# A 512-token trunk layer: the embedding product made by Strassen's scheme inside the output projection

## The chip, the core and the metric

The kernel runs on one NeuronCore of a Trainium2 chip. Five engines take part. TensorE (PE in the profile) multiplies into PSUM, which has eight banks of 128 x 512 fp32 values. VectorE (DVE) and ScalarE (ACT) work elementwise on SBUF and PSUM, GpSimd (POOL) issues DMAs with addition and does a little arithmetic, and SyncE (SP) issues plain DMAs. Each engine runs its own instructions strictly in program order and waits on semaphores for the others. The metric is the device time of one execution in microseconds. The kernel before takes 790.21 us (median of three runs, 790.07 to 790.22).

## The reference, cut to what matters

```python
D_MODEL, SEQ, PLE_DIM = 2048, 512, 256
def reference(x, p, ...):
    hn = rmsnorm(x, norm_g[0])
    x = x + swa_mixer(hn, ...)            # ends in (out * silu(gate)) @ w_out, 2048 x 2048
    emb = p[0] @ ple_proj[0]              # 512 x 256 @ 256 x 2048: the embedding
    g = sigmoid(rmsnorm(x, ple_norm[0]) @ ple_gate[0])   # 2048 x 2048: the gating product
    x = x + emb * g
    return rmsnorm(x, final_g)
```

All of it is fp32. The embedding `emb` needs only the inputs `p` and `ple_proj`, so it can be made at any time before the gating uses it.

## The kernel before, in words

**Products in three parts.** Each fp32 operand is split into a high half rounded to fp32r and a low half that holds the rest; `mm3` (L123) makes a product from three matmuls, high by high, high by low and low by high (L126 to L128 in the profile). A split costs one ACT cast and one DVE subtraction.

**Four large stages.** Input projections and attention come first (to about 450 us). The output projection `w_out` follows, then the gating product `ple_gate`, then the last rows with their stores. The output projection and the gating product are each done by a Strassen-like scheme of seven products of half size, in the order `ORDER_OUT = ORDER_PLE = (1, 7, 6, 5, 3, 4)` (L664) for six of them, and the seventh by a second level of small products (`SMALL`, L666: at which piece of which product a small one is put in). Product p has two column halves jj; a unit is written (p, jj), and has four pieces m = 0 to 3, so (6, 0, 1) is piece 1 of unit (6, 0). A piece is 128 x 1024 of weights, 512 KB, and feeds 12 matmuls 512 wide (`unit`, L997): two 128-row halves, two blocks of 128 tokens, three matmuls each. Units of products 6, 5 and 3 go on adding to the banks of product 1 (`chain`, L978).

**The pieces.** `Pieces` (L720) holds one list of specifications over both stages. When piece i is asked for (`get`, L779), `ahead` (L768) issues the DMA loads of the next three to six pieces on SP (L747, tile `braw`), and splits every piece up to i + 2: cast (L754, tile `bhi`) and subtraction (L755, tile `blo`). The tiles `bhi` and `blo` have three buffers each, so the cast of piece n waits until PE has finished piece n - 3. What is called piece n below is the n-th entry of this list: pieces 0 to 7 belong to product 1, 8 to 15 to product 7, and piece 16 opens product 6.

**Activation forms.** The moving side is the token operand, split the same way and formed as sums of quarters (`Forms`, L836; casts L867, subtractions L868, tiles `fho`/`flo` for the output projection, `fhg`/`flg` for the gating). They are made one product ahead, two buffers to the ring, so a form's cast waits for the piece that used its buffer last.

**The embedding.** `p` transposed is loaded and split once (L1205 to L1208, `pTh`, `pTl`). `ple_proj` comes as eight pieces of 128 x 2 x 512 in the same list, put between the units of the gating (`EMBEDS`, L827, `add_embeds`, L797). `embed` (L1211) makes a block of 128 tokens by 512 columns with 6 matmuls into a PSUM bank `e`. `gated` (L1217) takes the sigmoid on ACT (L1223), multiplies it by the bank on DVE (L1225), and adds the result to x, on DVE (L1229) or by an accumulating DMA on POOL (L1227). ACT then takes squares and their sums (L1240). The last four blocks are made in the tail by `block` (L1383), which multiplies by the pieces of product 4, then calls `embed`, for the tokens 256 to 511; the last of them is done in two strips of 288 and 224 columns on a bank that ACT has opened with the negative of what is to be subtracted (`opened_bank`, L1377).

**What sets the order.** In the output projection DVE, ACT and POOL follow a scheduler that reorders the instructions of each engine from the order of the code; from product 7 of the gating on, all engines follow the code (L1318). PE and SP follow the code throughout the stages in question here.

## Time and profile before

| what | value |
|---|---|
| median of three runs | 790.21 us (790.07 to 790.22) |
| the profiled execution, its own time | 789.45 us |
| its span, first to last instruction | 787.7 us |
| granted TensorE clock, mean | 0.996 |
| PE busy | 778.7 us, 99% |
| DVE busy | 607.9 us, 77% |
| ACT busy | 507.0 us, 64% |
| POOL busy | 139.6 us, 18% |
| output projection, first matmul of product 1 | at 450.57 us of the span |
| last matmul starts | at 779.3 us of the span |

The busy time of PE counts overlapping matmuls once: the matmuls are pipelined, one of 512 columns lasts about 0.39 us in the records and the next starts 0.23 us after it. Rows of the timeline read: start, duration, engine, line, operation, output and inputs, shape, and in brackets the idle time before it and what ended that. A row of the groups ends with the busy time, the mean of one in ns, and the idle time before. A row of the windows gives, for each engine in turn, busy us and instruction count, then the granted clock, the share of time that the 16 DMA engines are busy and GB/s.

### The profile page before, as it was taken

Reading aid. Unit: us, or ns where it says so; the run is one execution under the profiler, and the core shown is the slowest. Engines: PE = TensorE matmul, PEld = TensorE weight load, DVE = VectorE, ACT = ScalarE, POOL = GpSimd, SP = SyncE. Lnnn points to the kernel's source line nnn. Section 1 sums busy time; section 2 is a strip of 40 time slices with the busy share of each in tenths; the row PEclk is TensorE's granted clock in tenths of the full one; section 3 lists DMA queues with packets and bytes.
Section 4 is the critical chain, followed back from the end, with each engine's and each line's share of the span. In section 5 each row is a group of like instructions: output and inputs, shape, how many; then the busy total and the mean of one; then the engine's idle time right before and its main releaser. Section 6 shows DMA issues by size and latency. Waiting matters only on the chain. (4 is left out here: it accounts for less than half of the span.)

```text
span 787.7 us, 11098 instructions
## 1 busy us (share of the span) xinstructions
PE 778.7 (99%) x3726; PEld 651.8 (83%) x3726; DVE 607.9 (77%) x1037; ACT 507.0 (64%) x1064; POOL 139.6 (18%) x258
## 2 busy tenths in 40 slices
PE   9999999999999999999999999999999999999995
PEld 8888888888888888888888888888888888888885
DVE  4547697876877688777777898778879589877896
ACT  6743576666767576766666754456689666656953
POOL 0201423132223323122222200000000022202000
PEclk9999999999999999999999999999999999999998
DMA  9978999999999989999997489667873899979723
GB/s 346 294 206 298 194 274 298 292 280 269 280 275 258 271 232 309 256 289 263 282 258 197 136 320 383 207 209 238 270 265 108 292 290 262 247 239 251 208 86 129
DMA packets 47817, 198.07 MB, mean 251 GB/s; under 512 B 7104, under 2 KB 8128, under 8 KB 42000
## 3 DMA queue, kind: packets, MB, share of 16 engines
q1 hardware_dynamic: 38736, 151.95, 55.7%
q0 software_dynamic: 9024, 45.41, 30.0%
q8 instruction: 29, 0.48, 0.3%
q14 instruction: 28, 0.23, 0.1%
HBM read 189.16 MB, written 71.35 MB: 331 GB/s over the span
## 5 line engine op out<-in xcount | busy, mean ns | idle before, releaser
L755 DVE TENSOR_TENSOR blo<-braw,bhi 128x1024 fp32r<-128x1024 f32 x108 | 131.5, 1222 | 37.3 <-ACT bhi L754 36.4
L754 ACT CAST bhi<-braw 128x1024 fp32r<-128x1024 f32 x108 | 113.4, 1051 | 55.9 <-PE o L128 25.9
L126 PE MATMUL gps<-xh,whi 128*128 128x512 f32 x256 | 100.0, 390 | 0.0
L127 PE MATMUL gps<-xl,whi 128*128 128x512 f32 x256 | 99.9, 390 | 0.0
L128 PE MATMUL gps<-xh,wlo 128*128 128x512 f32 x256 | 99.7, 390 | 0.0
L126 PE MATMUL qps<-xh,whi 128*128 128x512 f32 x224 | 87.8, 392 | 0.0
L127 PE MATMUL qps<-xl,whi 128*128 128x512 f32 x224 | 87.4, 390 | 0.0
L128 PE MATMUL qps<-xh,wlo 128*128 128x512 f32 x224 | 87.3, 390 | 0.0
L110 DVE TENSOR_TENSOR wlo<-wraw,whi 128x1024 fp32r<-128x1024 f32 x60 | 73.5, 1227 | 2.8 <-ACT whi L109 2.7
L570 POOL TENSOR_SCALAR_AFFINE_SELECT own<-r 64x512 fp32r<-64x512 f32 (+1 forms) x48 | 32.5, 677 | 242.9 <-DVE r L560 237.2
L126 PE MATMUL o<-bhi,fho 128*128 128x512 f32 x192 | 74.8, 390 | 0.0
L128 PE MATMUL o<-bhi,flo 128*128 128x512 f32 x192 | 74.8, 389 | 0.0
L127 PE MATMUL o<-blo,fho 128*128 128x512 f32 x192 | 74.7, 389 | 0.0
L556 ACT CAST r<-pt 128x256 fp32r<-128x256 f32 x64 | 23.9, 374 | 68.8 <-PE pt L551 68.6
L109 ACT CAST whi<-wraw 128x1024 fp32r<-128x1024 f32 x60 | 62.3, 1040 | 4.6 <-issue 4.1
L126 PE MATMUL g<-bhi,fhg 128*128 128x512 f32 x160 | 62.7, 392 | 0.0
L128 PE MATMUL g<-bhi,flg 128*128 128x512 f32 x160 | 62.3, 389 | 0.0
L127 PE MATMUL g<-blo,fhg 128*128 128x512 f32 x160 | 62.3, 389 | 0.0
L128 PEld LDWEIGHTS gps<-xh,wlo 128*128 128x128 f32 x256 | 48.1, 188 | 10.3
L126 PEld LDWEIGHTS gps<-xh,whi 128*128 128x128 f32 x256 | 48.1, 188 | 9.1
L127 PEld LDWEIGHTS gps<-xl,whi 128*128 128x128 f32 x256 | 48.1, 188 | 8.8
L560 DVE TENSOR_TENSOR r<-pt,r 128x256 fp32r<-128x256 f32 x56 | 23.7, 424 | 41.0 <-ACT r L556 40.3
(244 smaller groups left out, 1789.3 us busy)
## 6 DMA issues: line engine op xcount, KB each, us to landing
wraw<-in_w_gate_in SPq DMA_DIRECT2D x32, 512.0 KB, 8.3
w_out<-in_w_out POOLq DMA_DIRECT2D x32, 512.0 KB, 9.0
braw<-w_out SPq DMA_DIRECT2D x32, 512.0 KB, 4.8
wraw<-in_w_q SPq DMA_DIRECT2D x28, 512.0 KB, 6.6
braw<-in_w_out SPq DMA_DIRECT2D x22, 512.0 KB, 4.1
braw<-in_ple_gate SPq DMA_DIRECT2D x22, 512.0 KB, 5.4
xw<-in_first SPq DMA_DIRECT2D x14, 640.5 KB, 6.7
w_out<-in_w_out SPq DMA_DIRECT2D x16, 512.0 KB, 10.2
```

Source lines behind the costliest of these rows:

```text
L109: nc.scalar.copy(hi, raw)
L110: nc.vector.tensor_sub(lo, raw, hi.bitcast(F32))
L126: nc.tensor.matmul(ps, sh, mh, start=first, stop=False, skip_group_check=more)
L127: nc.tensor.matmul(ps, sh, ml, start=False, stop=False, skip_group_check=more)
L128: nc.tensor.matmul(ps, sl, mh, start=False, stop=last, skip_group_check=more)
L556: nc.scalar.copy(rh, src)
L560: nc.vector.tensor_sub(rl, src, rh.bitcast(F32))
L570: nc.gpsimd.affine_select(out=flat(own), in_=flat(r).bitcast(F32), pattern=[[0, 8], [sign, HB]], compare_op=ALU.is_ge, fill=0.0, base=-HB ...
L754: nc.scalar.copy(hi, raw)
L755: nc.vector.tensor_sub(lo, raw, hi.bitcast(F32))
```

## The change

The eight `ple_proj` pieces, the split of `p` and the `e` banks leave the gating stage. A new class `Embedding` makes the same 512 x 2048 product inside the output projection, by Strassen's scheme with seven products in place of eight, in two column halves. Nine entries "emb" are put into the list of pieces, behind the pieces named in `EMBED_AT`: five of 1024 columns and four of 512. Their sums are prepared in the buffers `s1` and `s7` (free until the gating) by loads on SP, accumulating DMAs on POOL and four DVE additions (`embed_steps`); the forms of `p` are made in unit (7, 0) from `s2`. Each of the nine slots takes matmuls into pairs of banks from the tags "t" and "o", and sums are built by copying: ACT copies a bank into another bank (negated, to open it) or into SBUF. Each finished pair of blocks (128 x 2 x 512, 512 KB) is written to DRAM from `s2` by a POOL DMA (`keep`). There are 84 matmuls of 512 columns. In the gating each pair is loaded back by an SP DMA (`load_embeds`, tile tag "e", two buffers), at the pieces named in `embed_loads`, and the multiplication reads SBUF. The small products of the output projection move later (`SMALL`, `small_steps`). `fg` is allocated after product 3, since it shares its room with forms of `p`.

```diff
     SMALL = {
         "w_out": {
-            (5, 0): {1: [1], 3: [1]}, (5, 1): {1: [7], 3: [7]}, (3, 0): {1: [6], 3: [6]}, (3, 1): {1: [2], 3: [2]},
+            (5, 1): {2: [1], 3: [1]}, (3, 0): {0: [7], 1: [7], 3: [6]}, (3, 1): {0: [6], 1: [2], 3: [2]},
             (4, 0): {0: [5], 1: [5], 2: [4], 3: [4]}, (4, 1): {0: [3], 1: [3]},
...
             lo = wpool.tile([P, WE], F32R, tag="wlo", name=f"blo{i}")
-            nc.scalar.copy(hi, raw)
-            nc.vector.tensor_sub(lo, raw, hi.bitcast(F32))
+            n = raw.shape[-1]
+            nc.scalar.copy(hi[:, :n], raw)
+            nc.vector.tensor_sub(lo[:, :n], raw, hi[:, :n].bitcast(F32))
...
-                for of, j in EMBEDS.get((p, jj), ()) if nm == "ple_gate" else ():
-                    add_embeds(of, j)
         return at
 
     EMBEDS = {
-        (6, 1): [((1, 0), 0)], (5, 0): [((1, 1), 1), ((5, 0), 2)], (5, 1): [((5, 1), 3)],
-        (3, 0): [((3, 0), 2)], (3, 1): [((3, 1), 3)],
+        (6, 1): [(1, 0)], (5, 0): [(1, 1), (5, 0)], (5, 1): [(5, 1)], (3, 0): [(3, 0)], (3, 1): [(3, 1)],
     }
+
+    EMBED_AT = [
+        (6, 0, 1), (6, 0, 2), (6, 1, 0), (6, 1, 1), (6, 1, 3), (5, 0, 0), (5, 0, 2), (5, 0, 3), (5, 1, 1),
+    ]
...
-    fg = late.tile([P, D], F32, name="fg")
-    pTh = late.tile([P, 2, S], F32R, name="pTh")
-    pTl = late.tile([P, 2, S], F32R, name="pTl")
...
     small_steps = {
-        (6, 1, 2): 1, (5, 0, 0): 7, (5, 0, 2): 7, (5, 1, 0): 6, (5, 1, 2): 6, (3, 0, 2): 2, (3, 1, 0): 5, (3, 1, 2): 5,
+        (5, 0, 2): 1, (5, 1, 0): 7, (5, 1, 2): 7, (5, 1, 3): 6, (3, 0, 1): 6, (3, 0, 2): 2, (3, 1, 0): 5, (3, 1, 2): 5,
         (3, 1, 3): 4, (4, 0, 1): 3, (4, 0, 3): 3,
+    }
+
+    embeds = {
+        (c, jj): tc.dram_tile([P, 2, 512], F32, name=f"embeds{c}_{jj}") for c in (1, 5, 3, 4) for jj in range(2)
+    }
...
+            v1, v7 = flat(s1), flat(s7)
+            self.b1, self.b4, self.b5 = v7[:, :512], v7[:, 512:WE], v7[:, WE:]
+            self.b2, self.b3 = v1[:, :WE], v1[:, WE:]
+            self.to = [s2[:, n] for n in range(2)]
...
+            if step == "p":
+                load(self.to[1], a["pT"])
+            elif step == "forms":
+                self.make_forms()
+            elif step == "load0":
+                load(b4, src(1, 2, 0))
+                load(b31, src(2, 2, 0))
+                load(b1, src(1, 1, 0))
+                load(b20, src(2, 1, 0))
+            elif step == "sums0":
+                load(b50, src(2, 1, 0))
+                load(b51, src(1, 1, 1))
+                nc.vector.tensor_add(b30, b4, b31)
+                nc.vector.tensor_add(b21, b30, b1)
+                add(b4, src(1, 1, 0))
+                add(b50, b21)
+                B.base.update(zip(self.at, (b1, self.b2, self.b3, b4, b5)))
...
+        def times(self, q, piece, half, banks, first=False):
+            fh, fl = self.forms[q]
+            (bh, bl) = (v[half] for v in piece)
+            for tb in range(2):
+                mm3(banks[tb], fh[:, blk(tb)], fl[:, blk(tb)], bh, bl, first, True, True)
+
+        def bank_pair(self, name, tag):
+            return [bank(f"{name}{self.done}_{tb}", tag) for tb in range(2)]
+
+        def keep(self, c, jj, n, fill):
+            for tb in range(2):
+                fill(self.to[n][:, tb], tb)
+            nc.gpsimd.dma_start(embeds[c, jj], self.to[n])
+
+        def slot(self):
+
+            k = self.done
+            jj = 0 if k < 5 else 1
+            piece = B.get(self.at[k])
+            if k == 0:
+                self.left()
+            if k in (4, 8):
+                self.times(4, piece, 0, self.Z)
+                self.keep(4, jj if k == 8 else 0, 1, lambda to, tb: nc.scalar.copy(to, self.Z[tb]))
+            if k in (0, 4):
+                self.X = self.bank_pair("eX", "t")
+                self.times(1, piece, 1 if k else 0, self.X, True)
+                self.O = self.bank_pair("eO", "o")
+                for tb in range(2):
+                    nc.scalar.mul(self.O[tb], self.X[tb], -1.0)
+            elif k in (1, 5):
+                self.times(2, piece, 0, self.O)
+                self.times(6, piece, 1, self.X)
+                self.keep(1, jj, 0, lambda to, tb: nc.scalar.copy(to, self.O[tb]))
+                self.Y = self.bank_pair("eY", "o")
+                for tb in range(2):
+                    nc.scalar.copy(self.Y[tb], self.X[tb])
+            elif k in (2, 6):
+                self.times(7, piece, 0, self.Y)
+                self.times(3, piece, 1, self.X)
+                for tb in range(2):
+                    nc.scalar.copy(self.left_of[:, tb], self.Y[tb])
+                for tb in range(2):
+                    nc.scalar.copy(self.to[0][:, tb], self.X[tb])
+            elif k in (3, 7):
+                self.W = self.bank_pair("eW", "o")
+                self.times(5, piece, 0, self.W, True)
+                self.keep(5, jj, 1, lambda to, tb: nc.vector.tensor_add(to, self.W[tb], self.left_of[:, tb]))
+                self.keep(3, jj, 0, lambda to, tb: nc.vector.tensor_add(to, self.W[tb], to))
+                self.Z = self.bank_pair("eZ", "o")
+                for tb in range(2):
+                    nc.scalar.mul(self.Z[tb], self.left_of[:, tb], -1.0)
+            self.done += 1
+
+    embedding = Embedding(at_out["embed"])
+    embed_steps = {
+        (1, 1, 2): "p", (7, 0, 1): "forms", (7, 0, 3): "load0", (7, 1, 1): "sums0", (6, 0, 2): "load1", (6, 0, 3): "load2",
+        (6, 1, 0): "load3", (6, 1, 2): "sums1",
+    }
...
             def between(m, ps):
+                if (p, jj, m) in EMBED_AT:
+                    embedding.slot()
...
+                part = embed_steps.get((p, jj, step))
+                if part is not None:
+                    embedding.prepare(part)
...
-    pT = wpool.tile([P, WE], F32, tag="wraw", name="pT").rearrange("p (k t) -> p k t", k=2)
-    nc.sync.dma_start(pT, a["pT"])
-    nc.scalar.copy(pTh, pT)
-    nc.vector.tensor_sub(pTl, pT, pTh.bitcast(F32))
...
-    def embed(t, w, tag, c=slice(0, 512)):
-        e_ps = bank(f"e{t}_{done[t]}", tag)
-        for k in range(2):
-            mm3(e_ps[:, c], pTh[:, k, blk(t)], pTl[:, k, blk(t)], w[0][k][:, c], w[1][k][:, c], k == 0, k == 1)
-        return e_ps
-
-    def gated(t, j, zin, z, e_ps, c=slice(0, 512), share=1.0):
+    embed_of = {}
+
+    def load_embeds(c, jj):
+        t = embed_of[c, jj] = late.tile([P, 2, 512], F32, tag="e", name=f"e{c}_{jj}", bufs=2)
+        nc.sync.dma_start(t, embeds[c, jj])
+
+    embed_loads = {
+        (6, 1, 0): (1, 0), (6, 1, 2): (1, 1), (5, 0, 3): (5, 0), (5, 1, 3): (5, 1), (3, 0, 1): (3, 0), (3, 1, 1): (3, 1),
+        (3, 1, 3): (4, 0),
+    }
+
+    def gated(t, j, zin, z, e, c=slice(0, 512), share=1.0):
...
-        nc.vector.tensor_mul(z, e_ps[:, c], z)
+        nc.vector.tensor_mul(z, e[:, c], z)
...
+                if (p, jj, step) in embed_loads:
+                    load_embeds(*embed_loads[p, jj, step])
...
-            for (of, which), j in EMBEDS.get((p, jj), ()):
-                e = {}
-                w = B.get(at_ple["e", (of, which)])
-                for t in (2, 3) if of == 5 else (0, 1):
-                    e[t] = embed(t, w, "to"[which])
+            for of, which in EMBEDS.get((p, jj), ()):
+                e = {t: embed_of[of, which][:, t % 2] for t in ((2, 3) if of == 5 else (0, 1))}
...
-        e_ps = embed(2 + tb, w[jj], e_tag, c)
-        z = s2[:, jj, tb, c]
+        e, z = embed_of[4, jj][:, tb], s2[:, jj, tb, c]
...
+    load_embeds(4, 1)
```

The numbers behind an underscore in the following rows only keep tiles apart, and the number in `bhi15` is the piece's. In the kernel after, casts of pieces are L755 and those of forms L865.

First, ACT at the passage from product 7 to product 6 of the output projection, before. `fho5_00` to `fho5_11` are the four form casts of product 5; each waits for the piece that last used its buffer (`fho5_10` for piece 14).

```order
L754 CAST bhi13_5285<-braw13_5257 128x1024
L754 CAST bhi14_5308<-braw14_5281 128x1024
L867 CAST fho5_00_5431<-gate0_896 128x512
L754 CAST bhi15_5332<-braw15_5304 128x1024
L867 CAST fho5_01_5454<-gate0_896 128x512
L754 CAST bhi16_5356<-braw16_5259 128x1024
L867 CAST fho5_10_5497<-gate1_2333 128x512
L754 CAST bhi17_5374<-braw17_5283 128x1024
L867 CAST fho5_11_5520<-gate1_2333 128x512
L754 CAST bhi18_5392<-braw18_5306 128x1024
```

The same place after.

```order
L755 CAST bhi13_5306<-braw13_5278 128x1024
L755 CAST bhi14_5331<-braw14_5302 128x1024
L865 CAST fho5_00_5456<-gate0_896 128x512
L865 CAST fho5_01_5497<-gate0_896 128x512
L865 CAST fho5_10_5565<-gate1_2333 128x512
L755 CAST bhi15_5355<-braw15_5329 128x1024
L755 CAST bhi16_5383<-braw16_5280 128x1024
L755 CAST bhi17_5401<-braw17_5304 128x1024
L865 CAST fho5_11_5608<-gate1_2333 128x512
```

The casts of pieces 15 and 16 now stand behind `fho5_10`, where before they stood ahead of it.

Second, SP in the gating at the end of product 5, before (pieces 108 to 110 are the last of unit (5, 1), 112 is the first of product 3).

```order
L747 DMA braw109_7242<-ple_gate_5_1_2_832 128x1024
L747 DMA braw110_7262<-ple_gate_5_1_3_833 128x1024
L747 DMA braw111_7282<-in_ple_proj 128x2x512
L747 DMA braw112_7304<-in_ple_gate 128x1024
L747 DMA braw113_7330<-in_ple_gate 128x1024
L747 DMA braw114_7352<-in_ple_gate 128x1024
```

After, the numbers of the pieces are higher; 116 is the last of unit (5, 1) and 117 the first of product 3. `e5_0` is the first pair of the embedding for product 5, and takes the buffer that `e1_0` had.

```order
L747 DMA braw115_7398<-ple_gate_5_1_2_832 128x1024
L747 DMA braw116_7422<-ple_gate_5_1_3_833 128x1024
L1366 DMA e5_0_7445<-embeds5_0_5041 128x1024
L747 DMA braw117_7448<-in_ple_gate 128x1024
L747 DMA braw118_7471<-in_ple_gate 128x1024
L747 DMA braw119_7497<-in_ple_gate 128x1024
```

A load that waits for the second multiplication with `e1_0` on DVE now stands ahead of the loads of pieces 117 and 118.

Third, ACT from the casts of the first pieces of product 3 on, before.

```order
L1240 ACTIVATE s1_5039,ssq3_5038<-x1s_5033 128x512 x2
L754 CAST bhi113_7380<-braw113_7330 128x1024
L754 CAST bhi114_7400<-braw114_7352 128x1024
L1223 ACTIVATE s7_5041<-s7_5041,rstd2_6370 128x512
L867 CAST fhg4_00_7419<-hT0_6310 128x512
L762 CAST last0_7423<-grown72_6493 128x1024
L754 CAST bhi115_7429<-braw115_7378 128x1024
```

The same place after.

```order
L755 CAST bhi117_7499<-braw117_7448 128x1024
L755 CAST bhi118_7521<-braw118_7471 128x1024
L1379 ACTIVATE s7_5038<-s7_5038,rstd2_6595 128x512 x2
L1396 ACTIVATE s1_5036,ssq3_5035<-x1s_5033 128x512 x2
L755 CAST bhi119_7549<-braw119_7497 128x1024
L1379 ACTIVATE s7_5038<-s7_5038,rstd2_6595 128x512
L865 CAST fhg4_00_7568<-hT0_6535 128x512
L763 CAST last0_7572<-grown81_6714 128x1024
L755 CAST bhi120_7578<-braw120_7519 128x1024
```

Piece 112 of before is 117 of after. Two sigmoids and two squares now stand between the casts of the second and the third piece of unit (3, 0), and a sigmoid, a form and the first of the last pieces again before the fourth.

94 lines of the change are left out of this document (75 added, 19 removed).

## The prediction

> **What bounds the kernel now.** I read the page's busy times first, then the windows by stage, then the timeline where the change puts its work.
>
> ```profile
> PE 778.7 (99%) x3726; PEld 651.8 (83%) x3726; DVE 607.9 (77%) x1037; ACT 507.0 (64%) x1064; POOL 139.6 (18%) x258
> ```
> ```profile
> core 0: us, PE busy (x) PEld busy (x) DVE busy (x) ACT busy (x) POOL busy (x), PEclk, DMA share, GB/s
> 447.00:475.00 28.00, 28.00 (x126) 23.24 (x125) 27.95 (x33) 15.59 (x21) 2.12 (x2) 1.00 0.77 275
> 475.00:500.00 25.00, 25.00 (x112) 20.67 (x112) 22.18 (x27) 11.94 (x14) 0.00 (x0) 1.00 0.91 344
> 500.00:560.00 60.00, 60.00 (x266) 49.71 (x265) 46.65 (x52) 35.87 (x50) 0.00 (x0) 1.00 0.69 215
> ...
> 749.03:779.70 30.67, 30.57 (x163) 26.41 (x161) 28.26 (x47) 15.56 (x33) 1.91 (x3) 1.00 0.31 104
> ```
>
> The waits of PE over the whole span are one row, at the very start:
>
> ```profile
> PE warm_ps L141 <- PEq L1537: 0.9, 1, 0.9
> ```
>
> PE has no gap in any of these stretches: until 779.7 us every matmul follows the one before. So a matmul more costs its pitch, and a wait of PE, which now has none, costs its whole length. But in the last stretch DVE is busy for 28.26 of 30.67 us. There two engines are full at once, and taking work from one alone need not shorten it.
>
> **The change, term by term.** *Matmuls.* The embedding's own rows, ahead of 749.03 and from there on (L127 is a third of them):
>
> ```profile
> L127 PE MATMUL e<-blo,pTh x20: 389/389/389, 692.1 to 737.7; 128*128 128x512 f32 x20
> ...
> L127 PE MATMUL e<-blo,pTh x14: 273/389/389, 749.3 to 779.2; 128*128 128x512 f32 x10, 128*128 128x288 f32 x2, 128*128 128x224 f32 x2
> ```
> ```profile
> 488.63 0.62 ACT L867 CAST fho<-gate 128x512 fp32r<-128x512 f32 x1 [0.29 <-PE o L127]
> 488.65 0.39 PE L126 MATMUL o<-bhi,fho 128*128 128x512 f32 x1
> ...
> 491.35 0.62 ACT L867 CAST fho<-gate 128x512 fp32r<-128x512 f32 x1 [1.15 <-PE o L127]
> 491.37 0.39 PE L126 MATMUL o<-bhi,fho 128*128 128x512 f32 x1
> 491.60 0.39 PE L127 MATMUL o<-blo,fho 128*128 128x512 f32 x1
> 491.87 1.05 ACT L754 CAST bhi<-braw 128x1024 fp32r<-128x1024 f32 x1
> 492.95 1.23 DVE L755 TENSOR_TENSOR blo<-braw,bhi 128x1024 fp32r<-128x1024 f32 x1 [0.26 <-ACT bhi L754]
> ```
>
> The two PE rows at 488.65 and 491.37 open pieces 14 and 15 of the output projection: 12 matmuls in 2.72 us, a pitch of 0.227 us. The new scheme has 84 matmuls (7 products, 2 column halves, 2 token blocks, 3 parts), all where PE is full: +19.1 us. Removed are 60 early ones (3 x 20), 13.6 us, and 42 late ones: 30 wide at 0.227, 12 narrow at about 0.12 in proportion to their width, 8.2 us. Over the whole kernel that is 2.7 us less of PE. Whether the late 8.2 us come back is for DVE to say:
>
> ```profile
> 750.88 1.22 DVE L755 TENSOR_TENSOR blo<-braw,bhi 128x1024 fp32r<-128x1024 f32 x1
> 752.02 1.22 DVE L763 TENSOR_TENSOR low<-grown,last 128x1024 fp32r<-128x1024 f32 x1
> 753.15 1.22 DVE L755 TENSOR_TENSOR blo<-braw,bhi 128x1024 fp32r<-128x1024 f32 x1
> 754.29 0.68 DVE L1225 TENSOR_TENSOR s<-e,s 128x512 f32<-128x512 f32 x1
> ...
> 778.53 0.45 DVE L1472 TENSOR_TENSOR x1s<-x1s,fg 128x288 f32<-128x288 f32 x1
> 779.70 0.39 DVE L1225 TENSOR_TENSOR s<-e,s 128x224 f32<-128x224 f32 x1 [0.72 <-PE e L128]
> ```
>
> DVE runs here almost without a gap, and waits for PE once, for 0.72 us at the end. The last stores go out behind that work. What the change takes off DVE here are the subtractions of the last two embedding pieces (750.88 and 753.15, each 1.13 us to the next start) and that wait: 3.0 us come back. Bounds: 0.7 (the wait alone) and 8.2 (PE alone counts). I take 3.0 because DVE, not PE, has no room. Net: 19.1 - 13.6 - 3.0 = **+2.5 us** (-2.7 to +4.8).
>
> *Piece 15.* The order of ACT changes: the cast of piece 15 now stands behind `fho5_10`. The row at 491.35 is that form's cast: it waits for the second last matmul of piece 14, so it cannot move up. Today the cast and the subtraction behind it (491.87, 492.95) are those of piece 17, due later. In the new order the same two rows are those of piece 15, so its low half is ready at 492.95 + 1.23 = 494.18. PE needs it for the second matmul of piece 15, which now starts at 491.60. Stall: **+2.6 us**. Its load (two loads and two halves of `ple_proj`, 1 MB, are put ahead of it on SP) hides behind the same wait. Bounds: 2.3 and 3.0, by handoffs; piece 16 follows with 1 us in hand.
>
> *ACT copies and DVE sums.* The 28 bank copies are of this kind (the only rows of an ACT copy 512 wide out of PSUM):
>
> ```profile
> L1268 ACT ACTIVATE s<-g 128x512 f32<-128x512 f32 x4 | 2.3, 593 | 0.7 <-PE g L128 0.7
> ```
>
> 28 x 0.59 is 16.6 us. By the windows ACT has 13 us free in 475 to 500 and 24 us in 500 to 560. The cover is what a piece has in hand: that of piece 17 is ready at 494.18 by the rows above and needed at 491.60 + 2 x 2.72 = 497.04, so 2.9 us early. I cost the copies at nothing; a pair of them (1.2 us) ahead of a cast fits into the 2.9 us, two pairs and a sum do not quite, and then the piece behind is late. DVE is full in 447 to 475 and gets the form work of unit (7, 0): five operations of 512 columns (0.68) and five of 256,
>
> ```profile
> L560 DVE TENSOR_TENSOR r<-pt,r 128x256 fp32r<-128x256 f32 x56 | 23.7, 424 | 41.0 <-ACT r L556 40.3
> ```
>
> 5.5 us in all, spread over two units of 10.9 us each. I cost it at nothing, covered by the same 2.9 us and by DVE's 2.8 free us after 475; the upper end is 2.
>
> *Parking.* Each 512 KB store reads a buffer that ACT writes again. The squares of the output projection write the same `s2` and wait for the next to last store; the cast of a piece stands behind them on ACT. Near rows:
>
> ```profile
> braw<-in_ple_gate SPq DMA_DIRECT2D x22, 512.0 KB, 5.4
> ...
> braw<-small_ple_gate SPq DMA_DIRECT2D x8, 512.0 KB, 7.0
> ...
> x1s<-s POOLq DMA_DIRECT2D x8, 256.0 KB, 5.6
> ...
> out<-x1s SPq DMA_DIRECT2D x1, 512.0 KB, 3.5
> ```
>
> A store takes 3.5 to 5.6 us, from the sums of slot 7 to those squares PE runs two pieces and a slot, 5.4 to 6.8 us (a slot is 6 to 12 matmuls), and DVE's sums and another store come first. I take **+0.7 us** (0 to 4).
>
> *The gating.* The load of `e5_0` waits on SP until DVE is through with `e1_0`, and pieces 117 and 118 wait behind it. That product ends about 1 us after PE has done piece 112. The load of piece 117 then takes 5.4 to 7.0 us (the rows above), and one more load is ahead of it: 512 KB at 344 GB/s by 0.91 of the engines, 1.4 us where the engines are full, as they nearly are here. Behind it come, from these rows,
>
> ```profile
> L755 DVE TENSOR_TENSOR blo<-braw,bhi 128x1024 fp32r<-128x1024 f32 x108 | 131.5, 1222 | 37.3 <-ACT bhi L754 36.4
> L754 ACT CAST bhi<-braw 128x1024 fp32r<-128x1024 f32 x108 | 113.4, 1051 | 55.9 <-PE o L128 25.9
> ...
> L867 ACT CAST fhg<-hT 128x512 fp32r<-128x512 f32 x20 | 12.3, 613 | 4.7 <-DVE hT L855 2.6 <-PE g L127 2.1
> ...
> L1240 ACT ACTIVATE s<-x1s 128x512 f32<-128x512 f32 x15 | 9.4, 625 | 8.3 <-DVE x1s L1229 8.3
> ...
> L1223 ACT ACTIVATE s<-s,rstd 128x512 f32<-128x512 f32 x11 | 7.6, 718 | 6.9 <-DVE s L1399 5.0 <-DVE s L1274 1.9
> ...
> L1240 ACT ACTIVATION_READ_ACCUMULATOR s<-x1s 128x1 f32 x15 | 2.8, 186 | 0.0
> ...
> L1225 DVE TENSOR_TENSOR s<-e,s 128x512 f32<-128x512 f32 x15 | 10.0, 684 | 0.0
> ...
> L1274 DVE TENSOR_TENSOR s<-g,s 128x512 f32<-128x512 f32 x4 | 2.6, 682 | 0.0
> ```
>
> cast 1.05, subtraction 1.22, a product 0.68 and the read of the chain's bank 0.68, for which PE waits before it can go on with product 3 in that bank. In all 10.0 (without the load ahead) to 13.0 us, against the four pieces that PE has meanwhile, 10.9 us. Before, 12 to 24 embedding matmuls (2.7 to 5.4 us) stood between the units and gave room. I take the middle, 1.0 (0 to 2.1). From that read to the split of piece 120 runs a chain from ACT to DVE and back: two sigmoids 1.44, two squares 1.62, cast 1.05, subtraction 1.22, bank 0.68, sigmoid 0.72, form 0.61, two casts 2.10, subtraction 1.22, together 10.7, some 0.5 less since an operation starts before the one ahead of it is written back (1.13 against 1.22 in the DVE rows above), so 10.2 against three pieces and a matmul, 8.4 us: 1.8 (0, if the read comes early, to 3). Together **+2.8 us** (0 to 5).
>
> **Sum.** 2.5 + 2.6 + 0.7 + 2.8 = 8.6 us on the profiled execution's 789.45 gives 798.1. Its time is 0.76 below the median, so I predict 798.8 against 790.21.
>
> **Rivals.**
> *Faster by the count of matmuls.* One mechanism: DVE's tail is slack that only follows PE, so all 8.2 us come back, and loads and casts hide. Then 790.2 - 2.7 = 787.5. For it: PE is at 99%. Against it: DVE's rows above, and the order of ACT. It decides only if all stalls stay under 1.1 us. [...]
> *Covered gating.* Landings stay at 5.4 and squares wait for nothing: 790.2 + 2.5 + 2.6 = 795.3.
> *The clock falls in the new waits.*
>
> ```profile
> 779.70:781.00 1.30, 0.00 (x0) 1.00 0.00 0
> 781.00:782.00 1.00, 0.00 (x0) 1.00 0.00 0
> 782.00:783.00 1.00, 0.00 (x0) 0.55 0.00 0
> ```
>
> (PE alone: busy, clock, DMA.) Some 2.6 us after its last matmul the clock halves; piece 15's stall is as long, and a longer one may come before the last strip, where PE now runs ahead of the bank that ACT opens. The strip's 24 matmuls take 2.7 us and would take twice that; two falls add 1 to 5 us: 800 to 804. [...]
> *Longer waits on parking and form work.* The buffers of `s2` are written again within a piece or two; at slots 4 and 8 as well, each store could hold ACT 1 to 3 us: 802 to 806.
>
> **Chances.** The forecast (796.5 to 800) 0.47; covered gating or more of the tail returned (792 to 796.5) 0.20; clock or parking (800 to 806) 0.17, beyond that 0.05; faster by the count 0.06; in between, same, 0.05. A run of this kernel can tell about 0.2%, 1.6 us, from no change, so the same means 788.6 to 791.8. The range 792 to 806 leaves out 0.16. Faster 0.06, same 0.05, slower 0.89.
>
> **What would show it.** In the new profile: PE idle of about 2.6 us before piece 15 with the subtraction L756 as releaser; PE waits at the first matmuls of unit (3, 0), on DVE L1430, and at piece 120; `braw117` landing late on SP; no wait of DVE on PE in the tail, and PE idle ahead of the strip; no embedding matmul after 690 us. If PE shows no wait near piece 15, or the last DVE stretch shrinks by 8 us, I am wrong.

## The result, and the profile after

The changed kernel takes **811.26 us** (median of six runs, 808.18 to 813.35); the kernel before, run beside it, takes 789.84 us (six runs, 789.58 to 790.22). The ratio is 1.0265 (95% interval 1.024 to 1.029): 21.4 us slower. I had predicted 798.8, with a range up to 806. The sign was right; the loss is two and a half times as large as forecast. The profiled execution of the changed kernel took 812.43 us, of which 810.7 are its span, against 787.7 before.

The busy row of the page (to be read against the one of before):

```profile
PE 786.5 (97%) x3708; PEld 654.8 (81%) x3708; DVE 615.6 (76%) x1057; ACT 521.4 (64%) x1096; POOL 146.8 (18%) x270
```

There are 18 matmuls fewer, and yet PE is busy for 7.8 us more, and its span is 23.0 us longer. So the time is in gaps of PE and in matmuls that ran slower. The list of PE's waits had one row before. Now it has six more (waiting engine, tile and line, what ended the wait, total us, times, longest):

```profile
PE eO L126 <- ACT eO L1253: 4.1, 1, 4.1
PE open L126 <- ACT open L1535: 4.0, 1, 4.0
PE g L126 <- DVE s L1430: 2.5, 1, 2.5
PE g L127 <- DVE blo L756: 1.6, 3, 0.8
PE o L126 <- ACT bhi L755: 1.4, 1, 1.4
PE o L127 <- DVE blo L756: 1.2, 3, 0.8
```

Two of the windows of before, now of the changed kernel, and one more around the longest wait (columns as before: busy us of PE, PEld, DVE, ACT, POOL, then granted clock, DMA share, GB/s):

```profile
475.00:500.00 25.00, 22.58 (x98) 17.85 (x97) 24.36 (x35) 12.04 (x15) 1.74 (x2) 1.00 0.98 336
500.00:560.00 60.00, 55.94 (x238) 45.77 (x237) 36.23 (x44) 36.24 (x52) 5.51 (x9) 0.94 0.65 214
...
530.00:545.00 15.00, 10.94 (x39) 8.51 (x38) 4.85 (x6) 7.12 (x11) 1.07 (x2) 0.77 0.70 229
```

Before, PE was busy for 25.00 and 60.00 us in the first two stretches. In the second one the clock is no longer 1.00 throughout.

To see where the 23.0 us come from I cut the span at three matmuls: the first of product 1 of the output projection, the first of the gating product, and the first that uses the pieces kept for the end (tile `last`, the start of the tail).

| span of | output projection | gating | tail | time before them |
|---|---|---|---|---|
| before | 155.0 | 146.2 | 36.0 | 450.6 |
| after | 184.4 | 137.1 | 37.7 | 451.5 |
| difference | +29.4 | -9.0 | +1.7 | +0.9 |

The 0.9 us ahead of these stages stand already at the first matmul into the tile `ktps` (6.87 against 5.99 us): the matmuls at the start run slowly for longer (16 of them between 3 and 6 us, against 21). No work that the change adds or moves lies there. In the output projection 19.1 us are the 84 added matmuls; the other 10.3 are waits and slow matmuls. In the gating 72 matmuls left (16.3 us) but only 9.0 came back. I measured each gap by the distance from one matmul's start to the next, less the pitch of 0.227 us, so that the numbers below can differ by some tenths from the profile's idle times.

**Piece 15.** The timeline of the changed kernel:

```profile
492.59 0.39 PE L128 MATMUL o<-bhi,flo 128*128 128x512 f32 x1
492.79 0.62 ACT L865 CAST fho<-gate 128x512 fp32r<-128x512 f32 x1 [2.10 <-PE o L127]
493.31 1.99 ACT L755 CAST bhi<-braw 128x1024 fp32r<-128x1024 f32 x2
...
494.38 3.50 DVE L756 TENSOR_TENSOR blo<-braw,bhi 128x1024 fp32r<-128x1024 f32 x3 [0.25 <-ACT bhi L755]
494.40 0.50 PE L126 MATMUL o<-bhi,fho 128*128 128x512 f32 x1 [1.43 <-ACT bhi L755]
495.66 0.51 PE L127 MATMUL o<-blo,fho 128*128 128x512 f32 x1 [0.76 <-DVE blo L756]
```

The form's cast (492.79) stands ahead of the piece's cast (493.31), as the order said; PE waits 1.58 us for the high half (494.40 - 492.59 - 0.227) and 1.03 for the low half: 2.6 in all, as predicted.

**Slot 5, the longest wait.** DVE, POOL, ACT and PE in the order of time:

```profile
524.37 0.68 DVE L1271 TENSOR_TENSOR s<-eW,left_of 128x512 f32<-128x512 f32 x1
...
526.67 0.86 POOL L1189 DMA_DIRECT2D s<-s  x1 [6.78 <-DVE s L1272]
...
527.21 1.41 POOL L1236 DMA_DIRECT2D embeds<-s  x2
...
533.40 0.39 PE L128 MATMUL o<-bhi,flo 128*128 128x512 f32 x1
...
536.23 1.07 ACT L1247 COPY s<-eZ 128x512 f32<-128x512 f32 x2 [6.49 <-DMA embeds<-s]
537.19 1.09 ACT L1253 ACTIVATE eO<-eX 128x512 f32<-128x512 f32 x2
537.60 0.54 POOL L1236 DMA_DIRECT2D embeds<-s  x1 [8.98 <-ACT s L1247]
537.85 0.80 PE L126 MATMUL eO<-bhi,p_high 128*128 128x512 f32 x1 [4.06 <-ACT eO L1253]
```

The copy at 536.23, still of slot 4, parks the pair of product 4 in the buffer from which the pair of product 5 is still being stored. That store's sum was ready at 525.05 (524.37 + 0.68), its DMA was issued at 527.21 (POOL stood before it at 526.67 with an accumulating DMA that waited for DVE), and it landed at 536.15, 8.9 us later. Until then ACT did nothing; behind the copy stands the opening of the next bank (537.19), and PE waits for that: 4.2 us. Then the clock shows:

```profile
534.00:536.00 2.00, 0.00 (x0) 0.00 (x0) 0.00 (x0) 0.00 (x0) 0.00 (x0) 0.97 0.88 352
536.00:538.00 2.00, 0.15 (x1) 0.15 (x1) 0.00 (x0) 1.77 (x4) 0.40 (x1) 0.50 0.08 31
```

The clock halves about 2.1 us after the last matmul's end (533.8), and stays there for 5 us of matmuls. These came at 0.427 us instead of 0.227; with the first, slot 5 takes 2.4 us more for its twelve matmuls, 6.6 with the wait. The DMA engines are busy to 0.88 at the end of the store, with loads of pieces beside it; the page's medians say the same of the whole kernel (KB each, median us to landing):

```profile
braw<-in_ple_gate SPq DMA_DIRECT2D x22, 512.0 KB, 8.1
embeds<-s POOLq DMA_DIRECT2D x8, 512.0 KB, 5.7
e<-embeds SPq DMA_DIRECT2D x8, 512.0 KB, 9.9
```

`braw` took 5.4 before; `x1s` took 5.6 before and takes 9.2 now. A store's median is 5.7, just above the 3.5 to 5.6 that I had from the near rows; the one that PE waited for was one of the two slowest (8.9, and 9.6 for the store behind it).

**The gating.** SP, ACT, DVE and PE around the unit (3, 0):

```profile
736.64 0.32 SPq L1366 DMA_DIRECT2D e<-embeds  x1
...
737.07 3.91 SPq L747 DMA_DIRECT2D braw<-in_ple_gate  x4
...
743.53 1.05 ACT L755 CAST bhi<-braw 128x1024 fp32r<-128x1024 f32 x1 [2.42 <-DMA braw<-in_ple_gate]
...
744.62 1.22 DVE L756 TENSOR_TENSOR blo<-braw,bhi 128x1024 fp32r<-128x1024 f32 x1 [2.78 <-ACT bhi L755]
...
746.36 1.28 DVE L1430 TENSOR_TENSOR s<-g,s 128x512 f32<-128x512 f32 x2
...
747.19 0.49 PE L126 MATMUL g<-bhi,fhg 128*128 128x512 f32 x1 [2.48 <-DVE s L1430]
```
```profile
734.00:736.00 2.00, 2.00 (x11) 1.65 (x10) 1.81 (x3) 1.10 (x2) 0.00 (x0) 1.00 0.00 0
...
738.00:766.00 28.00, 24.09 (x96) 18.49 (x95) 21.45 (x26) 20.23 (x34) 6.55 (x9) 0.94 1.06 304
```

The load of `e5_0` holds SP until 736.64, and four loads of pieces come out behind it at once. From 734 to 736 the DMA engines did nothing; from 738 to 766 they are full (share 1.06). `braw117` lands after 6.4 us, the next three after 8.6, 11.0 and 13.1. So ACT waits for a load, DVE for ACT, the read of the chain's bank (L1430) comes late, and PE waits 2.65 us; at four other pieces, one of them earlier, it waits some 0.3 to 1.0: 5.0 us of gaps in the gating, and 1.8 more because the clock halved behind the long one.

**The tail.** PE waits 4.0 us for the last strip's bank, and its 24 matmuls run at half clock:

```profile
796.75 0.55 PE L126 MATMUL open<-last,fhg 128*128 128x224 f32 x1 [4.03 <-ACT open L1535]
```
```profile
797.00:800.00 3.00, 3.00 (x15) 3.00 (x16) 2.18 (x5) 2.07 (x5) 0.00 (x0) 0.50 0.92 300
```

DVE waits for that strip's sigmoid on ACT for only 0.7 us, as it had waited 0.72 us for PE before. But DVE has more left to do. From the first matmul of the tail to the end, before and after (DVE is the third number):

```profile
751.75:787.74 35.99, 27.85 (x151) 24.15 (x149) 28.00 (x51) 14.59 (x30) 2.45 (x4) 0.92 0.35 117
```
```profile
773.02:810.73 37.71, 25.16 (x121) 21.70 (x119) 29.22 (x53) 16.14 (x34) 2.44 (x4) 0.84 0.42 140
```

PE's work in the tail is smaller, and DVE's is larger by 1.2 us, although it has no subtractions of `ple_proj` any more: more of what DVE does for the gating is still to come when the tail begins (eight sums of x with the gated embedding in place of seven, and four low halves of the last pieces in place of three).

### The profile page after: what moved, and what is told of

The parts are those of the page before. It is cut to its first block, busy times and chain, and to the rows that moved or that the text cites. A ratio compares the mean times of both kernels' runs of the same rounds, so it can differ in the third digit from the quotient of the medians.

```text
span 810.7 us, 11171 instructions
## 1 busy us (share of the span) xinstructions
PE 786.5 (97%) x3708; PEld 654.8 (81%) x3708; DVE 615.6 (76%) x1057; ACT 521.4 (64%) x1096; POOL 146.8 (18%) x270
## 5 line engine op out<-in xcount | busy, mean ns | idle before, releaser
L756 DVE TENSOR_TENSOR blo<-braw,bhi 128x1024 fp32r<-128x1024 f32 x100 | 121.4, 1220 | 42.4 <-ACT bhi L755 41.8
L755 ACT CAST bhi<-braw 128x1024 fp32r<-128x1024 f32 x100 | 104.4, 1050 | 41.8 <-PE o L128 16.3
L128 PEld LDWEIGHTS gps<-xh,wlo 128*128 128x128 f32 x256 | 48.1, 188 | 10.3
L529 ACT ACTIVATE t<-t,sm 128x129 f32<-128x129 f32 (+1 forms) x128 | 49.6, 389 | 8.7 <-DVE sm L525 7.3
```

The costliest lines, as they stand in the source:

```text
L128: nc.tensor.matmul(ps, sl, mh, start=False, stop=last, skip_group_check=more)
L529: nc.scalar.activation(su, su, AF.Exp, bias=sm[:, u : u + 1], accum_out=sm[:, 2 + u : 3 + u])
L755: nc.scalar.copy(hi[:, :n], raw)
L756: nc.vector.tensor_sub(lo[:, :n], raw, hi[:, :n].bitcast(F32))
```

## The experiments

Every kernel below ran in three rounds beside the kernel before. The theory, after the reading above: three waits that the clock makes longer (parking in one buffer, the order of ACT at piece 15, SP held by a load), on top of matmuls that came back in part only. The rivals are those of the prediction, and that the lost time is spread over many small things. Single executions of the changed kernel differ by 5 us (808.18 to 813.35, mean clock 0.992 to 0.986), and in the traces the clock falls behind a wait in one and not behind the same wait in another (1.00 and 0.50 behind piece 15, experiment 3); so beside the medians I give what the profiled execution shows in the stretch that an edit touches.

**1. Another buffer for the parked pair.** The pair of product 4 goes out of `left_of`, whose last reader is the copy itself, and not out of the buffer that is still being stored.

```diff
             self.left_of = late.tile([P, 2, 512], F32, tag="spare", name="left_of")
+            self.to.append(self.left_of)
...
-                self.keep(4, jj if k == 8 else 0, 1, lambda to, tb: nc.scalar.copy(to, self.Z[tb]))
+                self.keep(4, jj if k == 8 else 0, 2, lambda to, tb: nc.scalar.copy(to, self.Z[tb]))
```

> The changed kernel, but the pair of product 4 is parked from the buffer left_of, which is free there, and not from the s2 half whose store to DRAM takes 8.94 us. Theory (each wait stands by itself on PE): the wait of PE in slot 5 (4.2 us) goes, and with it the 2.5 us that its 12 matmuls lose at half clock: 811.3 - 6.7 = 804.6 us, clock 1.00 from 530 to 560. Rival (the DMA engines are full, and the next late transfer stops PE instead): a wait of some 3 us at one of the next pieces, 808 to 811 us.

Measured: 804.82 us (ratio to before 1.0193, 1.0178 to 1.0208), 6.4 us less than the changed kernel. The wait on `eO` is gone, and with it the slow clock (the stretch 530 to 560 us, where the changed kernel had 25.94 and 0.89):

```profile
530.00:560.00 30.00, 29.83 (x133) 24.38 (x132) 19.85 (x24) 21.92 (x36) 2.67 (x5) 1.00 0.74 261
```

The wait and the slow matmuls behind it, 4.2 + 2.4 = 6.6 us by the trace, are shown to be the price of parking in that buffer: the output projection takes 177.9 us here, 6.5 less.

**2. The order of ACT at piece 15.** One loading step of the embedding moves behind the cast.

```diff
-        (1, 1, 2): "p", (7, 0, 1): "forms", (7, 0, 3): "load0", (7, 1, 1): "sums0", (6, 0, 2): "load1", (6, 0, 3): "load2",
+        (1, 1, 2): "p", (7, 0, 1): "forms", (7, 1, 0): "load0", (7, 1, 1): "sums0", (6, 0, 2): "load1", (6, 0, 3): "load2",
```

> The changed kernel, but the four first loads of ple_proj are issued one piece later, at (7, 1, 0), behind the load of piece 15; the cast of piece 15 then stands ahead of fho5_10 on ACT again. Theory: the 2.6 us wait at piece 15 goes, 808.7 us. Rival (the load is late, not the cast): piece 15 or slot 0 waits for a landing, 810 to 812 us.

Measured: 807.03 us (1.0221, 1.0205 to 1.0236), 4.2 us less. The wait at piece 15 is gone from PE's list (0.4 us in two small ones is left). That is 1.6 more than the wait itself. In the profiled execution piece 15 costs 2.5 us less; slot 5 kept 3.8 us of wait, but its slow stretch was half as long (3.4 us against 6.8), in a place that the edit does not touch. The order of ACT, which the step's place decides, is shown to be the cause of the wait at piece 15.

**3. The held load.** The DMA of `e5_0` is issued two pieces later, at (5, 1, 1), when the buffer is free; the tile is allocated where it was.

```diff
-        nc.sync.dma_start(t, embeds[c, jj])
+        if (c, jj) != (5, 0):
+            nc.sync.dma_start(t, embeds[c, jj])
...
+                if (p, jj, step) == (5, 1, 1):
+                    nc.sync.dma_start(embed_of[5, 0], embeds[5, 0])
```

> The changed kernel, but the DMA that loads e5_0 is issued at (5, 1, 1), behind the loads of pieces 117 to 119, so that nothing on SP is held while DVE still reads e1_0. Theory (the held queue is the cause): the DMA engines are no longer idle at 734 to 737 us, the wait at the first matmul of unit (3, 0) (2.6 us) and the slow clock behind it (1.8 us) go, and about half of the 1.9 us at pieces 120 to 122: 806 us. Rival (the pairs are simply too many bytes for this stretch): landings stay at 9 to 13 us, the waits move, 809 to 811 us.

Measured: 806.91 us (1.022, 1.0204 to 1.0235), 4.4 us less. The wait on the chain's bank is gone, and with it the slow clock (1.00 from 700 to 760 us); what stays in the gating are three waits for low halves of pieces (2.4 us in all) and one of 0.9 on a high half. Those are longer than in the changed kernel, probably because the first wait had given the later pieces time there. So of the 4.4 us only about half belongs to the held load: the gating takes 134.9 us in the profiled execution, 2.2 less than in the changed kernel's (135.5 to 137.7 in the four profiles with the hold, 133.6 to 135.4 in the five without it). The rest comes from stretches that the edit does not touch: at slot 5 the wait was 3.1 us here and the clock stayed up (1.00 from 530 to 560 us, against 0.89). The rival came true in part, too: the loads of pieces behind `braw118` still land after 9.8, 11.0, 12.7 and 13.2 us.

In the same run the clock halved behind piece 15 (0.50 from 496 to 498 us), where it had not in the changed kernel (1.00), though the wait there is as long (1.43 and 0.76 us in both). The stretch 475 to 500 us has 98 matmuls in the changed kernel and 91 here, so the same wait costs 2.6 us in the one and 1.6 more (7 x 0.227) in the other. That fits the spread of the changed kernel's runs (5 us, against 0.6 before; mean clock 0.986 in the two slowest, 0.992 in the fastest).

**4. The wait kept, the clock held.** 19 bf16 matmuls of zeros are added to an open bank ahead of slot 5; they change no value.

```diff
+                for _ in range(19 if k == 5 else 0):
+                    nc.tensor.matmul(chain[0][0], fill0, row_of_ones, start=False, stop=False, skip_group_check=True)
                 self.times(2, piece, 0, self.O)
```

> The changed kernel with 19 matmuls of zeros (bf16, 512 wide, 0.21 us each, added into an open bank of product 1's chain) ahead of the matmuls of slot 5, where PE waits 4.2 us for ACT. The wait itself stays. Theory (the clock halves because PE is idle): the clock stays at 1.00 and 2.5 us come back, 808.8 us. Rival (the slow matmuls are slow for another reason, such as the copies that read the same banks): no change, 811 us, and the pitch of 0.43 us stays.

Measured: 809.23 us (1.0238, 1.0221 to 1.0255), 2.0 us less by the medians, but within the spread of the changed kernel's runs; what tells is the trace. ACT waits for the store as before, and the zeros fill PE's wait:

```profile
534.38 4.31 PE L1256 MATMUL o<-const-bfloat16-1.0,fill 128*128 128x512 bf16 x19
...
536.89 1.07 ACT L1247 COPY s<-eZ 128x512 f32<-128x512 f32 x2 [6.41 <-DMA embeds<-s]
```
```profile
530.00:560.00 30.00, 30.00 (x135) 22.99 (x134) 17.13 (x22) 17.46 (x27) 2.13 (x4) 1.00 0.65 227
```

Slot 5 now costs 4.3 us beyond its matmuls instead of 6.6, and these come at 0.227 us again. So 2.3 us were the clock, which stays at 1.00 here with PE's wait filled, and the rest is the wait itself. (In the execution profiled here the clock halved behind piece 15, as in experiment 3: 0.50 from 496 to 498 us.)

**5 and 6. What the tail can give back.** In the kernel before I leave out the 30 embedding matmuls behind 751 us (the multiplication reads an x1 tile instead), and in a second kernel also the two `ple_proj` pieces that they use, with their loads, casts and subtractions.

```diff
-        e_ps = embed(2 + tb, w[jj], e_tag, c)
+        e_ps = x1[jj][:, 2 + tb, :]
```

> The kernel before without the 30 embedding matmuls of the last four blocks (18 wide, 12 narrow, 5.5 us of PE); the multiplication reads x in SBUF in place of the bank, so that part of the output is not the layer's. Everything else stays, the casts and subtractions of the two last ple_proj pieces too. Theory (DVE and ACT set the tail): 0 to 1 us faster, 789 to 790. Rival (PE sets it): 5.5 us faster, 784.3.

> As the run before, and the two last ple_proj pieces are left out too, with their loads, casts and subtractions. The prediction's sum has 2.3 us for the two subtractions and 0.7 for the wait at the end: 786.8. Rival by the changed kernel's trace (the chain from ACT to DVE behind unit (3, 1) sets the tail, and the subtractions lay beside it): about 1 us in all, 788.8.

Measured: 788.46 us (0.9988, 0.9979 to 0.9998) and 787.07 us (0.9965, 0.9951 to 0.9979). 5.5 us less of PE's work (18 x 0.227 + 12 x 0.12) bring 1.2 us; two splits less bring another 1.4. Together 2.6 to 2.8 (by the medians of before, 789.63, and by the span, 787.7 - 784.9). So PE does not set the tail, and the 3.0 of the prediction was right as a price in the kernel before. That it is DVE, and not ACT, is argued from busy times (28.00 and 14.59 of the 36.0 us of the tail before), and not shown: experiment 6 leaves out casts and loads as well as subtractions.

**7. The three mended together.** The edits of 1, 2 and 3 in one kernel.

> The three edits together on the changed kernel: the pair of product 4 parked from left_of, the first ple_proj loads one piece later, the load of e5_0 behind those of pieces 117 to 119. Theory (separate waits): the three gains of 6.4, 4.2 and 4.4 us add up, 811.3 - 15.0 = 796.3. Rival (they share a cause and shift to each other): 799 to 801.

Measured: 799.16 us (1.0116, 1.0097 to 1.0135), where the single gains add up to 15.0 us and 796.3. By stages the three do add up: 6.5 us of the output projection in 1, 2.5 at piece 15 in 2 and 2.2 of the gating in 3 are 11.2, and the span is 11.6 us shorter here (799.1 against 810.7; output projection 9.0, gating 1.7). The medians of 2 and 3 held more than their edits, as said there. What is left waits at three pieces of product 3, 741 to 747 us.

**8. And the last strip filled.** As 7, with 19 matmuls of zeros ahead of the last strip.

```diff
+    fill_ps = bank("fill", "t")
+    for _ in range(19):
+        nc.tensor.matmul(fill_ps, fill0, row_of_ones, start=True, stop=True, skip_group_check=True)
     last = block(1, 1, "s", upper, 1.0 / D, upper_ps)()
```

> The three edits together, and 19 matmuls of zeros into a free bank ahead of the last strip, where PE waits 4 us for the bank that ACT opens and then runs at half clock. Theory (DVE ends the tail and waits only 0.7 us for the strip): the clock stays up there, 0.7 us faster than without the zeros. Rival (PE's strip ends the tail): 2.7 us faster.

Measured: 798.56 us (1.0111, 1.0096 to 1.0126): 0.6 less, though PE's 3.5 us wait and the slow strip are gone; the runs of 7 spread by more than that (796.97 to 800.80). It fits that DVE waits for that strip for 0.7 us only.

**9. Hardly any loads.** The edits of 1 and 2, and six of the eight loads of embeddings left out (their places take the first pair, so the output is not the layer's).

```diff
+        if c != 1:
+            embed_of[c, jj] = embed_of[1, jj]
+            return
```

> The changed kernel with the pair of product 4 parked from left_of and the first ple_proj loads one piece later, and with six of the eight loads of the embedding left out in the gating: after the first two pairs the multiplication reads these again, so the output is not the layer's. No load is held on SP, and 3 MB less move. The run with three edits, which still loads all pairs, has 799.2 us, and PE waits some 4.3 us (with the slow clock) at pieces 118 to 122. Theory (the DMA engines are full there, casts wait for landings): 4 to 5 us faster than that run, 794.5. Rival (the chain between ACT and DVE sets it): 1.8 us of waits stay at piece 120, 796.5.

Measured: 797.37 us (1.0094, 1.0079 to 1.0109), 1.8 us less than 7; theory and rival both expected more. The waits of 7 are still there:

```profile
738.00 1.05 ACT L755 CAST bhi<-braw 128x1024 fp32r<-128x1024 f32 x1 [1.58 <-DMA braw<-in_ple_gate]
...
740.94 0.72 ACT L1383 ACTIVATE s<-s,rstd 128x512 f32<-128x512 f32 x1 [1.89 <-DVE s L1434]
...
745.57 0.79 PE L127 MATMUL g<-blo,fhg 128*128 128x512 f32 x1 [0.96 <-DVE blo L756]
```

ACT waits here once for a piece (which had been under way for 9.7 us, though the loads of embeddings are gone) and once for DVE's read of the bank. Both stand in the chain that the prediction named; the traffic of the parked pairs is not the main part of it, since the DMA engines are full without it (share 1.05 from 728 to 746 us). POOL's transfers run there too: a 512 KB load and four of the accumulations into `x1s`, issued from 727 to 737 us, take 9.4 to 11.5 us each.

**10. The early matmuls alone.** In the kernel before the 72 embedding matmuls between the units and just ahead of the tail are left out (any SBUF values take their place in the multiplication); the `ple_proj` pieces are still loaded and split.

```diff
-                    e[t] = embed(t, w, "to"[which])
+                    e[t] = fg[:, :512]
```

> The kernel before without its 72 embedding matmuls between the units of the gating (16.3 us of PE); the multiplication reads fg in their place, so the output is not the layer's. All pieces of ple_proj are still loaded and split, so the bytes and the work of ACT and DVE are as before. Theory (these matmuls were also the time in which loads land and ACT and DVE work): PE waits for the rest, and only some 9 to 11 us come back, 779 to 781. Rival (the cover was not needed): 16.3 us, 773.3.

Measured: 789.95 us, the same as before (1.0002, 0.9992 to 1.0011), where PE has 16.3 us less to do; neither the theory nor the rival had that. The gating gets 1.9 us shorter and the tail 1.6 longer. PE, which had waited for nothing, now waits for splits:

```profile
PE g L127 <- DVE blo L755: 6.2, 5, 3.3
PE g L126 <- ACT bhi L754: 2.8, 2, 1.5
```

and the clock drops behind those waits (40 us of the gating, PE busy for all of them before):

```profile
690.00:730.00 40.00, 34.14 (x139) 26.58 (x138) 30.73 (x36) 23.91 (x32) 5.23 (x6) 0.96 0.89 245
```

The count of matmuls at 0.227 us is right for what is added to a full PE, and wrong for what is taken away: the embedding matmuls were also the time in which pieces land (ACT waits once for 1.4 us on a load) and in which ACT and DVE split them.

**11. The whole embedding left out.** As 5, 6 and 10 together: no pieces of `ple_proj`, no splits, no embedding matmul.

> The kernel before with the whole embedding left out of the gating and the tail: no pieces of ple_proj, no loads, casts or subtractions of them, no embedding matmuls (102, 21.9 us of PE); fg and x stand in for it in the multiplications, so the output is not the layer's. This is the most that taking the embedding out of there can give. The prediction's sum: 13.6 + 2.7 us between the units and about 3 us with the tail, 773.3 (789.6 - 16.3). Theory after the runs so far (ACT, DVE and the DMAs hold PE once the cover is gone): about 12 us, 777.5. Full count of the matmuls: 767.7.

Measured: 776.38 us (0.9834, 0.9817 to 0.985): 13.2 us less, for 102 matmuls (21.9 us) and eight pieces less. The gating now gives 15.6 of its 16.3 us, with no wait in it; the tail takes 1.5 us longer, with PE waiting 3.6 us for the last strip's bank.

13.2 us is what comes back from the gating and the tail when the embedding there costs nothing and nothing else is changed. The changed kernel spends 19.1 on its matmuls in the output projection (20.5 with the small waits that experiment 8 kept). By these numbers this form of the change is 6 to 7 us slower than before even without its long waits. That is no firm bound: the tail here takes 37.5 us, where that of experiment 6, which also has no embedding in it, took 33.2. If the 15.6 us of the gating and the 2.8 of experiment 6 could be had together, 18.4 would come back, and 1 to 2 us would be lost: an estimate, which no run here shows.

**12. Splits of the last pieces later.** As 8, with the first two of the pieces kept for the tail split one step later, to shorten the chain ahead of pieces 118 to 120.

```diff
-    early = {(3, 0, 0): 0, (3, 0, 2): 1, (3, 1, 0): 2, (3, 1, 1): 3, (3, 1, 2): 4, (3, 1, 3): 5}
+    early = {(3, 0, 1): 0, (3, 0, 3): 1, (3, 1, 0): 2, (3, 1, 1): 3, (3, 1, 2): 4, (3, 1, 3): 5}
```

> The changed kernel with the three edits and the zeros ahead of the last strip (798.6 us), and besides the first two of the last pieces are split one step later, at (3, 0, 1) and (3, 0, 3), so that a cast and a subtraction less stand ahead of piece 120. Theory (the chain between ACT and DVE sets the wait there): the waits at piece 120 (1.1 and 1.2 us) shrink by 1.0 to 2.0, 797. Rival (the landings set it): no change, 798.6.

Measured: 798.98 us (1.0117, 1.0102 to 1.0132), against 798.56: nothing. One wait shrank from 1.1 to 0.3 us, the others stayed or grew, and the casts wait for loads, once for 1.56 us and three times for less:

```profile
736.84 1.05 ACT L755 CAST bhi<-braw 128x1024 fp32r<-128x1024 f32 x1 [1.56 <-DMA braw<-in_ple_gate]
```

So the splits of the last pieces are not what holds those pieces. How the rest of these waits (3.5 us of gaps in experiment 8) divides between late loads and the chain of ACT and DVE stays open.

No version here beats the kernel before.

## Why the prediction was right and where it failed

| term of the sum | predicted | profiled execution | what tells it |
|---|---|---|---|
| 84 matmuls in the output projection | 19.1 | 19.1 | pitch 0.227 outside the slow stretches |
| piece 15 | 2.6 | 2.6 | rows at 494.40 and 495.66, experiment 2 |
| copies and sums of ACT and DVE | 0 (to 2) | 0.8 | two gaps of 0.4 us |
| parking | 0.7 (0 to 4) | 6.6 | 4.2 of wait, 2.4 of clock; experiments 1 and 4 |
| 72 matmuls out of the gating | -13.6 and part of -3.0 | -16.3 | |
| waits in the gating | 2.8 (0 to 5) | 6.8 | 5.0 of waits, 1.8 of clock; the gaps of the trace (experiment 3 gives back 2.2) |
| tail, without the 12 matmuls ahead of it | rest of -3.0 | +1.7 | DVE's 29.22 us against 28.00; experiments 5, 6 and 8 |

With the 0.9 us ahead of the stages and 0.8 us of small delays (the matmul after each wait for a low half comes 0.1 us late) the right column makes the 23.0 us. The forecast was 8.6, so 14.4 us were missed: 5.9 by the term for parking, 4.0 by the one for the gating, 2.0 in what the removed matmuls and splits give back, 0.8 by the copies, and 1.7 for which there was no term. The time came out above the whole range, because parking and the gating both went beyond their upper ends (4 and 5 us) at once.

- **Where it slows down: right.** Piece 15, the wait on L1430 at the first matmuls of (3, 0), `braw117` landing late, the later wait near piece 120, PE idle ahead of the strip: each was foretold by its place and its releaser, and each is in the trace. Piece 15 is right to a tenth, since all its rows stood in the trace of before.
- **Parking: the term that failed most.** The step said "a store takes 3.5 to 5.6 us" and put against it the 5.4 to 6.8 us that PE runs from the sums of slot 7 to the squares (by its own counts two pieces and a slot are 30 to 36 matmuls, 6.8 to 8.2 us). I looked at the wrong use of the buffer for the sum: the squares waited for nothing (ACT does them at 563.08 us, right behind the copy of slot 8). The use that bit is in slot 4, where the pair of product 4 is copied into the buffer of product 5's pair; PE feels it at the first matmul of slot 5. And the duration was taken from medians. This store was issued behind an accumulating DMA and landed after 8.9 us, with the DMA engines full (share 1.00 over its time). The rival "longer waits on parking" had named slots 4 and 8, and 1 to 3 us each: the mechanism was that rival's, and slot 4 was right, but ACT was held for 6.5 us there, and at slot 8 not at all.
- **The clock: a rival that came true beside the forecast.** I gave it 1 to 5 us as a case of its own, by estimate: two falls, of which only the strip's 2.7 us of matmuls stood in a trace. The size was right, but it is no case of its own: it comes on top of waits. It took 2.4 us at slot 5, 1.8 in the gating, and a strip at half speed that costs at most 0.6 (experiment 8). Experiment 4 shows it apart from the wait. (By the row in the prediction the clock fell 2.4 us after the last matmul's end, not 2.6.) Nor does it follow from the wait alone: piece 15's, 1.43 and 0.76 us, left the clock at 1.00 in the changed kernel, and the same wait halved it in experiments 3 and 4 (the last section has the rows).
- **The gating: right places, too small.** The term was 1.0 for the held load and 1.8 for the chain. Behind the held load I priced the load of piece 117 with "one more load ahead of it", 1.4 us. In fact five loads came out within 4 us, the engines had stood idle for 2 us before and were full for 28 after, and each later piece landed later (6.4, 8.6, 11.0, 13.1). I had priced the piece behind the hold, not the queue behind it. But the hold is only a third of the loss: without it the gating takes 2.2 us less (experiment 3), and the late landings and some 4 us of waits stay. Those are shared between late loads and the chain of ACT and DVE; how, stays open (experiments 9 and 12).
- **The count: right, for the wrong reason in part.** "60 early ones, 13.6 us" is nearly what the gating gives if the splits go too (experiment 11: 15.6 of 16.3), and the change does take those splits away. But experiment 10 shows that the matmuls alone give nothing. "3.0 us come back" in the tail is confirmed in the kernel before by experiment 6 (2.6 to 2.8). In the changed kernel the tail and the 12 matmuls ahead of it gave 1.0 (-2.7 + 1.7), and with the strip's wait filled about 0.6 more. The step that failed is that DVE's other work in the tail stays what it was. DVE has 29.22 us there, where experiment 6, which leaves out the same splits, has 25.79: the shorter gating hands on work that it had covered. And the 0.7 us wait at the end, which the sum let go, is still there.
- **Faster by the count: not borne out.** Its mechanism, a tail that only follows PE, is excluded by experiment 5 (1.2 us for 5.5). In experiment 11 13.2 us come back, against 19.1 put in. By busy time PE is the fullest engine, with 99% and its weight loads at 83% against DVE's 77%; experiment 10 relieves it of 16.3 us, and the time stays the same.

Experiment 8, which has neither piece 15's wait nor the one on parking, comes out at 798.6, my predicted time. That is chance: it lacks 2.6 us that I had counted, and keeps more of the waits in the gating.

## What to carry to other kernels

Work that fills an engine at 99% may be the cover of the engines beside it: what it gives back when it is removed is measured by leaving it out together with the work that it covers (16.3 us of matmuls gave nothing here alone, and 15.6 in the gating with the splits), and what it cost where it was added is its full pitch (84 times 0.227 us), so the two sides of such a move cannot be set off by their counts. A buffer that is stored and written again was a wait of one store in the worst traffic of that stage, not in the median one (8.9 us against 5.7); and a load that waited at the head of a queue delayed the four behind it and let them out within 4 us, to land after 6.4 to 13.1. PE's waits of 4.06 and 2.48 us came with half the clock here, and cost 2.4 and 1.8 us of slow matmuls beyond their own length; two of 0.93 and 0.95 us, one matmul apart, were followed by it in experiment 7, and nearly the same two in experiment 8 were not. And what an edit gives is read in the stretch that it touches: where the clock falls behind a wait in one trace and stays up behind the same wait in another, a median of few runs mixes the edit with that.

## What the runs showed of the hardware

- In the changed kernel's trace the clock was at 0.50 in four stretches: from 535.89 to 542.71, from 747.51 to 750.93 and from 795.30 to 802.13 us of the span, and from 805.54 us to the end. The first and the third began within a wait of PE (4.06 and 4.03 us long), the second 0.32 us behind the end of one (2.48 us), and the last when PE had no matmul left.
- The same wait halved the clock in one trace and not in another. At piece 15 PE waited 1.43 and 0.76 us both in the changed kernel and in experiment 3. The changed kernel (PE is the first number behind the length, the clock the third from the end):

```profile
494.00:496.00 2.00, 0.84 (x2) 0.48 (x3) 1.75 (x3) 2.00 (x3) 0.86 (x1) 1.00 1.04 363
496.00:498.00 2.00, 2.00 (x10) 1.68 (x9) 2.00 (x3) 0.25 (x1) 0.00 (x0) 1.00 1.07 306
```

Experiment 3:

```profile
494.00:496.00 2.00, 1.24 (x5) 0.99 (x5) 2.00 (x3) 1.40 (x2) 0.17 (x1) 0.88 1.08 326
496.00:498.00 2.00, 2.00 (x6) 1.54 (x6) 1.04 (x1) 0.00 (x0) 0.00 (x0) 0.50 1.08 305
```

- So with two short waits. In experiment 7 PE waited 0.93 and 0.95 us, one matmul apart (up to 745.44 and 746.90 us), and the clock fell behind them:

```profile
735.00:755.00 20.00, 17.37 (x66) 13.14 (x66) 14.85 (x19) 15.00 (x28) 4.04 (x6) 0.91 1.06 313
```

In experiment 8 it waited 0.97 and 0.95 us at the same place (up to 744.37 and 745.82 us), and the clock stayed:

```profile
735.00:755.00 20.00, 17.28 (x72) 12.81 (x71) 15.64 (x19) 15.88 (x28) 3.60 (x5) 1.00 1.05 306
```

What decides between the two is not shown here.

- A POOL store of 512 KB took 2.9 us where the DMA engines had just run empty (issued at 537.60, share 0.08 in the 2 us around it) and 8.9 us ten microseconds earlier, with the engines full (share 1.00).
